# Entry to a gated MLP on one NeuronCore: order of evictions and sums, arithmetic moved from GpSimd to VectorE, six differences put off, the fourth product one step back

## The chip, the core and the metric

The kernel runs on one core of a Trainium2 chip. The metric is the time of one execution on the device in microseconds, given as the median of several runs. The engines are named as the profile names them: PE is TensorE (PEld its weight loads), DVE is VectorE, ACT is ScalarE, POOL is GpSimd, SP the engine that issues most of the DMAs. Each engine works through its own queue in order and waits on semaphores of the others.

## What is computed

One layer of a decoder trunk over 1024 tokens of width 1024, all in float32: a token mixer (causal pooling and gated linear attention) and then a gated MLP with a causal convolution of width 3, each behind a root-mean-square norm that is scaled and shifted by a conditioning vector. The change lies at the end of the first part and in the second:

```python
        y = jnp.concatenate([y_pool, y_gla], axis=-1) @ w_out[l]
        x = x + g1[:, None, :] * y

        h = modulate(rmsnorm(x), sh2, sc2)
        x = x + g2[:, None, :] * conv_ffn(h, w_up[l], conv_w[l], conv_b[l], w_down[l])
    return rmsnorm(x) * final_norm

def conv_ffn(h, w_up, conv_w, conv_b, w_down):
    up = h @ w_up
    y = causal_conv_width_3(up, conv_w) + conv_b
    a, b = jnp.split(y, 2, axis=-1)
    return (jax.nn.silu(a) * b) @ w_down
```

The MLP's inner width `D_FF` is 2816, that is 22 blocks of 128 channels for `a` and 22 for `b`.

## The kernel before

Everything is held transposed: channels on the 128 partitions, tokens along the row. The 1024 tokens are two halves (`hf` 0 and 1) of `T` = 512. A float32 product is made of three matmuls of split operands: each operand is cut into a high part (a cast by ScalarE) and a low part (a subtraction by VectorE, the `wl`, `ws` and `xs` rows of the profile), and `mm3` adds high by high, high by low and low by high.

**Up-projection.** For block `i` of the 22, the four quarter problems (halves of the tokens by the blocks `a` and `b`, over two halves of the inner dimension) are done with seven products instead of eight, in the manner of Strassen and Winograd. A product is 12 matmuls. The kinds are numbered 1 to 7: kinds 1 and 2 accumulate in a bank `x`, 5 and 3 in a bank `z`, and `y` is started with a copy of product 1 (`seeded`) and accumulates 6, 7 and 4. `up_step(kind, i)` issues one product and what follows it:

- after 5 and 6, ScalarE copies the bank out (`u[5]`, `u[6]`);
- after 3 and 7, VectorE adds bank and copy into `cb` (the eviction of line 944); after 7 the convolution of `cb` follows (`conv`: one ScalarE and two VectorE instructions) and gives `yb`;
- after 4, ScalarE copies `y` into `ca`; then come the convolution of `ca`, SiLU on ScalarE, the product with `yb` on VectorE (line 996) and a store of the result to DRAM, `gd[i]`, issued by GpSimd;
- last, for the first 11 blocks, GpSimd takes the difference of the two halves of the gated result and stores it (`s3d`); for the other 11 it loads the second half of block `i - 11` again, adds the second half of this one, and stores that (`s1d`). The down-projection reads both.

`order` is the order of the products on TensorE, which is written out by hand: TensorE's queue keeps it (`manual_schedule`). The queues of the other engines are ordered by a planner from priorities and its own estimate of when operands are ready; `issue_after` puts an instruction behind another on its engine. The first `RAMP` = 6 blocks begin with their products 1 and 2, which need the first half of the tokens alone, while the operands of the others are still being made from the second half (`norm2_second`, two steps of it after each product). Then the six blocks get their products 5, 4 (of the block before), 6, 3, 7. The other 16 blocks run with seven products each. `prepare` makes the weights' operands four products ahead: the load of raw weights (`up_raw`, four buffers of 512 KB), the differences of weights that Strassen's scheme needs (line 812) and the split (`wsplit`, lines 801 and 802).

**Entry.** Before it, `jobs_out(1)` is the output projection for the second half of the tokens: four banks at a time, and after each bank's last matmul `evac(d, pp)`: VectorE evicts the bank with gate and residual into `x1` (line 693), SP stores it, for `d` from 4 on VectorE adds the scaled quarter operands into `sums` (line 698), ScalarE squares it and GpSimd adds the square to `nacc` (line 234, by `sumsq_step`; the last square is not added but goes to TensorE by itself). `rstd_of` sums `nacc` over the channels with TensorE and makes the norm factor with ScalarE (`Ln`, then `Exp`). The banks of `jobs_out` are handed on to the MLP (`psum["f"]`, eight banks).

**Buffers.** `cy` gives six tiles of 1024 columns for `ca`, `cb`, `yb` and the gated result; `small` gives seven of 512 columns for the copies and the reloaded halves.

**Down-projection.** After the last block the same kind of scheme runs over `gd`, `s1d`, `s3d` and `w_down`. Its first products are mixed with product 4 of the last block; its tiles lie where those of the up-projection were.

## Time and profile before

| | us |
|---|---|
| median of 3 runs | 1050.42 |
| lowest and highest | 1049.86, 1051.85 |
| the profiled execution | 1047.94 |
| its span | 1046.2 |
| TensorE busy in it | 1001.2 |
| VectorE busy | 854.6 |
| ScalarE busy | 549.2 |
| GpSimd busy | 190.5 |

The span runs from the first to the last instruction of the profiled execution. In rows of the timeline the first number is the start in microseconds, the second the duration; then engine, line, operation, output and inputs by the program's names, shapes and the count of merged instructions; in brackets the idle time of the engine before it and what ended it. In rows of waits the numbers are the total, the count and the longest. In rows of groups the two numbers behind the bar are the sum in microseconds and the mean in nanoseconds, then the idle time before them.

### The profile page before, as it was taken

The page shows a single profiled execution, that of the slowest core. Times are in us where ns is not written, and L with a number is a line of the kernel's source. Part 1 is how long each engine was busy: PE and PEld are TensorE (multiplying, and loading weights), DVE is VectorE, ACT ScalarE, POOL GpSimd, SP SyncE. Part 2 cuts the span into 40 slices and gives each one's busy share as a digit, 9 for nine tenths or more (in the row PEclk, how much of TensorE's full clock was granted, in tenths as well). Part 3 has the DMA queues.
Part 4 walks back from the last instruction along what each step waited for, and adds up shares of the span by engine and source line. Part 5 has one row for each costly group of instructions (what it writes and reads, how often), then busy time and mean ns, then how long its engine had stood idle before and what let it go on. Part 6 is the DMA issues. An engine that isn't in the chain of part 4 may idle for free.

```text
span 1046.2 us, 12684 instructions
## 1 busy us (share of the span) xinstructions
PE 1001.2 (96%) x4481; PEld 815.4 (78%) x4481; DVE 854.6 (82%) x1197; ACT 549.2 (52%) x888; POOL 190.5 (18%) x163
## 2 busy tenths in 40 slices
PE   7989999998999989999999999999999999999995
PEld 5768868886777768877888888888888788888874
DVE  7967899689988849999977788777776776988883
ACT  5465585442733547665555455555554544644442
POOL 3437203222141030011100101101001000200210
PEclk8999999999999999999999999999999999999998
DMA  8743232455487442233222222332334787223642
GB/s 315 258 151 111 81 110 83 149 174 182 149 280 262 155 167 81 86 137 129 105 99 91 105 102 107 131 111 101 111 111 151 272 283 240 101 81 111 201 141 81
DMA packets 60817, 154.21 MB, mean 147 GB/s; under 512 B 6641, under 2 KB 9809, under 8 KB 60754
## 3 DMA queue, kind: packets, MB, share of 16 engines
q1 hardware_dynamic: 54192, 134.00, 37.8%
q0 software_dynamic: 4928, 17.30, 4.3%
q10 hardware_dynamic: 1634, 2.10, 0.6%
q8 instruction: 35, 0.57, 0.2%
q14 instruction: 28, 0.23, 0.1%
HBM read 127.69 MB, written 25.69 MB: 147 GB/s over the span
## 4 chain that ended last, share of the span: by engine, by line
PE 62%; DVE 23%; DMA 5%; ACT 4%; issue 4%; POOL 2%; SPq 0%; POOLq 0%; ACTq 0%; DVEq 0%
PE dn L107 18%; PE upy L107 14%; PE upx L107 9%; PE upz L107 9%; PE pp L107 8%; DVE wl L153 3%; DVE ada L219 2%; DMA ada<-in_adaT_dram 2%; DVE xs L802 2%; DVE hl L275 2%; POOL le L347 1%; DVE la L376 1%; DVE ua L812 1%; DVE lq L359 1%; PE ss L107 1%
## 5 line engine op out<-in xcount | busy, mean ns | idle before, releaser
L107 PE MATMUL dn<-xs 128*128 128x512 f32 (+1 forms) x480 | 111.1, 386 | 1.7 <-DVE xs L802 1.3
L107 PE MATMUL dn<-ws 128*128 128x512 f32 x456 | 108.3, 394 | 2.3 <-DVE xs L1110 2.3
L107 PEld LDWEIGHTS dn<-xs 128*128 128x128 f32 x480 | 88.5, 188 | 21.1 <-DVE xs L802 2.1
L107 PEld LDWEIGHTS dn<-ws 128*128 128x128 f32 x456 | 86.7, 190 | 20.9 <-issue 2.7
L107 PE MATMUL upy<-sh,xs 128*128 128x512 f32 x264 | 86.6, 390 | 2.1 <-DVE cb L944 2.1
L107 PE MATMUL upy<-sh,ws 128*128 128x512 f32 x264 | 86.4, 389 | 0.0
L153 DVE TENSOR_TENSOR wl<-raw,wh 128x1024 fp32r<-128x1024 f32 (+1 forms) x50 | 64.2, 1285 | 27.1 <-ACT wh L152 26.8
L997 POOL DMA_DIRECT2D gd<-y x22 | 12.0, 546 | 375.7 <-DVE y L996 358.7
L107 PE MATMUL pp<-hh,wh 128*128 128x512 f32 x176 | 73.7, 419 | 2.7 <-ACT hh L274 1.4
L107 PE MATMUL pp<-hl,wh 128*128 128x512 f32 x176 | 70.8, 402 | 4.8 <-DVE hl L275 4.8
L107 PE MATMUL pp<-hh,wl 128*128 128x512 f32 x176 | 70.8, 402 | 2.6 <-DVE wl L153 2.6
L802 DVE TENSOR_TENSOR xs<-ua,xs 128x512 fp32r<-128x512 f32 x78 | 60.6, 782 | 14.8 <-ACT xs L801 14.8
L802 DVE TENSOR_TENSOR ws<-ua,ws 128x512 fp32r<-128x512 f32 x76 | 55.1, 727 | 15.7 <-ACT ws L801 15.7
L107 PE MATMUL upx<-hh,xs 128*128 128x512 f32 x192 | 62.8, 392 | 2.5 <-DVE x L693 2.5
L801 ACT CAST ws<-ua 128x512 fp32r<-128x512 f32 x76 | 47.0, 622 | 34.4 <-PE upy L107 17.2
L152 ACT CAST wh<-raw 128x1024 fp32r<-128x1024 f32 (+1 forms) x50 | 50.4, 1008 | 26.8 <-DMA raw<-in_w_out_dram 10.8
L801 ACT CAST xs<-ua 128x512 fp32r<-128x512 f32 x78 | 48.1, 622 | 30.5 <-PE upy L107 17.4
L812 DVE TENSOR_TENSOR ua<-ua 128x512 f32<-128x512 f32 x88 | 60.2, 687 | 2.1 <-DMA ua<-in_w_up_dram 0.3
L347 POOL TENSOR_TENSOR le<-b 128x512 f32<-128x512 f32 x24 | 37.1, 1549 | 134.1 <-DVE lq L359 53.8
L107 PE MATMUL upz<-sh,ws 128*128 128x512 f32 x184 | 60.4, 389 | 0.0
L937 DVE SCALAR_TENSOR_TENSOR y<-ca,vec,y 128x1023 f32<-128x1023 f32 (+1 forms) x44 | 56.3, 1280 | 4.3 <-ACT y L934 3.5
L107 PEld LDWEIGHTS upy<-sh,xs 128*128 128x128 f32 x264 | 49.5, 188 | 13.2 <-DVE cb L944 2.9
(261 smaller groups left out, 2521.2 us busy)
## 6 DMA issues: line engine op xcount, KB each, us to landing
ua<-in_w_up_dram SPq DMA_DIRECT2D x49, 512.0 KB, 3.4
ada<-in_adaT_dram SPq DMA_DIRECT2D x32, 512.0 KB, 3.4
gd<-y POOLq DMA_DIRECT2D x22, 512.0 KB, 2.9
raw<-in_w_qkru_dram SPq DMA_DIRECT2D x18, 512.0 KB, 3.3
da<-gd SPq DMA_DIRECT2D x36, 256.0 KB, 2.8
da<-in_w_down_dram SPq DMA_DIRECT2D x36, 256.0 KB, 3.4
raw<-in_w_out_dram SPq DMA_DIRECT2D x16, 512.0 KB, 4.4
x<-in_xT_dram SPq DMA_DIRECT2D x24, 256.0 KB, 4.3
```

What stands on the lines that cost most here:

```text
L107: pe.matmul(out=out, lhsT=lhsT, rhs=rhs, start=start, stop=stop, skip_group_check=more)
L152: act.copy(out=wh, in_=raw)
L153: dve.tensor_tensor(out=wl, in0=raw, in1=wh.bitcast(F32), op=ALU.subtract)
L219: dve.scalar_tensor_tensor(out=a, in0=a, scalar=1.0, in1=cb, op0=ALU.mult, op1=ALU.mult, accum_out=acc)
L275: mark["split"] = dve.scalar_tensor_tensor(out=l, in0=t, scalar=sh, in1=h.bitcast(F32), op0=ALU.add, op1=ALU.subtract)
L347: pool_e.tensor_tensor(out=e.rearrange("p (n h) -> p n h", n=nb), in0=b.rearrange("p (n h) -> p n h", n=nb), in1=bb[:, :, 0, h - 1:h].broa ...
L359: dve.tensor_tensor(out=ql.rearrange("p e (n h) -> p e n h", h=h), in0=q2.rearrange("p e (n two h) -> p e n two h", two=2, h=h)[:, :, :, 1 ...
L801: act.copy(out=h, in_=src)
L802: dve.tensor_tensor(out=l, in0=src, in1=h.bitcast(F32), op=ALU.subtract)
L812: eng.tensor_tensor(out=out, in0=a, in1=b, op=ALU.subtract)
L937: dve.scalar_tensor_tensor(out=y[:, sh:], in0=c[:, :S - sh], scalar=cw[j], in1=y[:, sh:], op0=ALU.mult, op1=ALU.add)
L997: nc.gpsimd.dma_start(out=gd[i], in_=ya)
```

## The change

In the entry, the four sums are issued together after the last eviction, and the additions of squares for `d` from 4 to 6 go to VectorE. The order on TensorE changes: in the ramp 5, 6, 4, 3, 7 instead of 5, 4, 6, 3, 7; in the later blocks 1, 5, 4, 2, 6, 3, 7 instead of 1, 4, 5, 2, 6, 3, 7 (product 4 is always that of the block before). What follows the convolution of `ca` (SiLU, gate product, store, difference or addition) is put off by `gated()` to the start of the next product 5 or 6, with SiLU behind the latest seed copy on ScalarE. Differences and additions of gated halves are done by VectorE. For the first six blocks the difference is left out at first; it is made six blocks later from two halves loaded from `gd`. SiLU's table is loaded right behind the norm factor's `Exp`. `norm2_second` starts after the second product instead of the first.

```diff
-        act.activation(out=r, in_=r, func=AF.Exp, scale=-0.5)
+        mark["exp"] = act.activation(out=r, in_=r, func=AF.Exp, scale=-0.5)
...
-            if hf and d >= 4:
-                sums[d - 4] = up_pool.tile([P, T], F32, tag="a22", name="s1", bufs=10)
-                dve.scalar_tensor_tensor(out=sums[d - 4], in0=x1[1][d],
-                                         scalar=modv[:, 32 + d:33 + d], in1=x1[1][d - 4],
-                                         op0=ALU.mult, op1=ALU.add)
...
-            nacc[hf] = sumsq_step(nacc[hf], d, x1[hf][d], pool_e, True, own)
+            nacc[hf] = sumsq_step(nacc[hf], d, x1[hf][d], dve if hf and d >= 4 else pool_e,
+                                  True, own)
+            if hf and d == 7:
+                for e in range(4):
+                    sums[e] = up_pool.tile([P, T], F32, tag="a22", name="s1", bufs=10)
+                    dve.scalar_tensor_tensor(out=sums[e], in0=x1[1][4 + e],
+                                             scalar=modv[:, 36 + e:37 + e], in1=x1[1][e],
+                                             op0=ALU.mult, op1=ALU.add)
...
     for i in range(NFF):
-        order += [(1, i)] if i >= RAMP else [(5, i)]
-        order += [(4, i - 1)] if i else []
-        order += [(5, i), (2, i)] if i >= RAMP else []
-        order += [(6, i), (3, i), (7, i)]
+        done = [(4, i - 1)] if i else []
+        if i < RAMP:
+            order += [(5, i), (6, i)] + done + [(3, i), (7, i)]
+        else:
+            order += [(1, i), (5, i)] + done + [(2, i), (6, i), (3, i), (7, i)]
...
         r = rstd_of(nacc[1], s2)
+        with tc.issue_after(mark["exp"].ins):
+            act.preload_act_table_set("silu_and_others")
...
-        act.copy(out=y, in_=src)
+        mark["seed"] = act.copy(out=y, in_=src)
...
         if kind == 5 and i < RAMP:
             u["y"] = seeded(u["s"], w[0][:, 0] if i < 3 else None)
+        if kind in (5, 6):
+            gated()
...
             ya = conv(u["ca"], i)
-            last = act.activation(out=ya, in_=ya, func=AF.Silu)
+            pend.append((i, ya, u["yb"]))
+            del st_u[i]
+            if i == NFF - 1:
+                gated()
+
+    def gated():
+        while pend:
+            i, ya, yb = pend.pop(0)
+            with tc.issue_after(mark["seed"].ins):
+                last = act.activation(out=ya, in_=ya, func=AF.Silu)
             if i == NFF - 1:
                 exp_ln(last)
-            dve.tensor_tensor(out=ya, in0=ya, in1=u["yb"], op=ALU.mult)
+            dve.tensor_tensor(out=ya, in0=ya, in1=yb, op=ALU.mult)
             nc.gpsimd.dma_start(out=gd[i], in_=ya)
-            if i < NFF // 2:
-                sub(pool_e, u["yb"][:, 0:T], ya[:, 0:T], ya[:, T:])
-                nc.gpsimd.dma_start(out=s3d[i], in_=u["yb"][:, 0:T])
+            if RAMP <= i < 2 * RAMP:
+                a, b = small("s3"), small("s3")
+                nc.sync.dma_start(out=a, in_=gd[i - RAMP][:, 0:T])
+                nc.sync.dma_start(out=b, in_=gd[i - RAMP][:, T:])
+                sub(dve, a, a, b)
+                nc.gpsimd.dma_start(out=s3d[i - RAMP], in_=a)
+            if i < RAMP:
+                pass
+            elif i < NFF // 2:
+                sub(dve, yb[:, 0:T], ya[:, 0:T], ya[:, T:])
+                nc.gpsimd.dma_start(out=s3d[i], in_=yb[:, 0:T])
             else:
                 t = small("s1")
                 nc.sync.dma_start(out=t, in_=gd[i - NFF // 2][:, T:])
-                pool_e.tensor_tensor(out=t, in0=t, in1=ya[:, T:], op=ALU.add)
+                add_to(t, t, ya[:, T:])
                 nc.gpsimd.dma_start(out=s1d[i - NFF // 2], in_=t)
...
-        for _ in range(2):
+        for _ in range(2 if n else 0):
             next(second, None)
```

## The prediction

> **What bounds the kernel now.** I read the page first: TensorE works 96% of the span, so only its idle time can be won, and a change to other engines counts where TensorE waits.

> ```profile
> span 1046.2 us, 12684 instructions
> PE 1001.2 (96%) x4481; PEld 815.4 (78%) x4481; DVE 854.6 (82%) x1197; ACT 549.2 (52%) x888; POOL 190.5 (18%) x163
> ```

> Next, busy times by stage: entry and ramp of the MLP (386 to 482), the steady up-projection (to 810), the step into the down-projection (to 830), its first part. The first two numbers of a row are its window and length; then TensorE, weight loads, VectorE, ScalarE, GpSimd.

> ```profile
> 386.00:482.00 96.00, 91.43 (x398) 74.08 (x397) 94.34 (x128) 61.53 (x99) 12.27 (x12) 1.00 0.31 106
> 482.00:810.00 328.00, 328.00 (x1448) 271.38 (x1447) 258.36 (x311) 176.28 (x261) 43.43 (x54) 1.00 0.32 111
> 810.00:830.00 20.00, 18.32 (x79) 14.29 (x78) 13.79 (x15) 11.31 (x16) 2.40 (x3) 1.00 0.70 234
> 830.00:975.00 145.00, 145.00 (x642) 120.05 (x641) 118.37 (x180) 71.15 (x128) 13.24 (x7) 1.00 0.51 169
> ```

> TensorE loses 4.57 us in the first window, 1.68 in the third, nothing in the other two, at a granted clock of 1.00. So 6.25 us is the ceiling of any gain here. VectorE is full in the ramp (94.34 of 96) and has 69.6 us free in the steady stage. TensorE's waits name the places:

> ```profile
> PE upx L107 <- DVE x L693: 2.5, 1, 2.5
> PE upy L107 <- DVE cb L944: 2.1, 2, 1.2
> PE dn L107 <- DVE xs L802: 1.3, 1, 1.3
> PE dn L107 <- ACT xs L801: 0.4, 1, 0.4
> ```

> All but the last wait for VectorE. The timelines of the three places follow, each beside the part of the change that touches it.

> **Part 1, the entry: evictions ahead of sums, three adds from GpSimd to VectorE.**

> ```profile
> 384.78 1.43 DVE L693 SCALAR_TENSOR_TENSOR x<-pp,modv,x 128x512 f32<-128x512 f32 x2 [2.38 <-PE pp L107]
> 385.57 1.37 ACT L230 ACTIVATE nsq<-x 128x512 f32<-128x512 f32 x2
> 386.13 2.42 DVE L698 SCALAR_TENSOR_TENSOR s<-x,modv,x 128x512 f32<-128x512 f32 x2
> 386.34 3.34 POOL L234 TENSOR_TENSOR nsa<-nsa,nsq 128x512 f32<-128x512 f32 x2 [14.81 <-ACT nsq L230]
> 386.39 0.39 PE L107 MATMUL pp<-yh,wl 128*128 128x512 f32 x1
> 388.47 1.40 DVE L693 SCALAR_TENSOR_TENSOR x<-pp,modv,x 128x512 f32<-128x512 f32 x2
> 389.27 0.50 PE L107 MATMUL upx<-hh,xs 128*128 128x512 f32 x1 [2.48 <-DVE x L693]
> ```

> The first MLP matmul starts at 389.27, when the third eviction ends (388.47 plus half of the pair, 0.7). That eviction queues behind two sums of 2.42 us, stretched by GpSimd's adds: a pair of evictions, operations of the same kind, takes 1.40, so the stretch is about 1.0. Without the sums the third eviction follows the pair at 386.2 and ends at 386.9; TensorE, whose last matmul ends at 386.78, goes on at 387.0. Gain 389.27 - 387.0 = 2.3 us. The bounds: the moved adds (0.68 each, the price of a VectorE addition of that size below) may enter between the evictions, because their squares (the ScalarE pair from 385.57) are ready by then: two of them leave 1.0; the whole wait is 2.48. I take 2.3: the third eviction becomes ready at 386.2, about when the first square does. The four sums then follow; their reader needs the norm factor, which comes after the adds and one product later in TensorE's order than now.

> The stage's VectorE account: three adds are 3 x 0.68 = 2.0 us more; gone are two stretches at the sums, about 2.1 us. It comes out even.

> **Part 2, the ramp: six GpSimd half-differences go, the fourth product goes one step back.**

> ```profile
> 462.33 0.39 PE L107 MATMUL upy<-sh,xs 128*128 128x512 f32 x1
> 463.82 2.20 DVE L802 TENSOR_TENSOR xs<-ua,xs 128x512 fp32r<-128x512 f32 x1
> 464.16 1.30 POOL L812 TENSOR_TENSOR y<-y 128x512 f32<-128x512 f32 x1
> 465.94 0.68 DVE L944 TENSOR_TENSOR cb<-upy,u 128x512 f32<-128x512 f32 x1
> 466.67 0.50 PE L107 MATMUL upy<-sh,xs 128*128 128x512 f32 x1 [1.24 <-DVE cb L944]
> 481.41 0.50 PE L107 MATMUL upy<-sh,xs 128*128 128x512 f32 x1 [0.85 <-DVE cb L944]
> ...
> 487.14 2.72 PE upz L107 x12
> ...
> L802 DVE TENSOR_TENSOR xs<-ua,xs 128x512 fp32r<-128x512 f32 x15 | 13.3, 895 | 0.0
> L802 DVE TENSOR_TENSOR ws<-ua,ws 128x512 fp32r<-128x512 f32 x15 | 11.7, 781 | 0.0
> ...
> 435.33 0.59 ACT L951 COPY upy<-sp 128x512 f32<-128x512 f32 x1 [0.84 <-PE upy L107]
> ```

> Product 7 ends at 462.72. Its eviction (L944) reads the bank that product 4 goes on accumulating in, so TensorE may not start product 4 before it. It runs at 465.94, behind a weight split that takes 2.20 us while GpSimd's difference runs (1.30) and 0.68 otherwise: 1.52 lost. The two groups of splits between 395 and 482 show three such blocks (gate products 0 to 2): 13.3 + 11.7 - 30 x 0.68 = 4.6 us of VectorE. Without its own block this eviction would end at 465.1. And product 4 starts one product later, 2.7 us of further grace. Against both stands that TensorE comes 2.3 us earlier from part 1. Balance: needed at 466.67 - 1.24 - 2.3 + 2.7 = 465.8; there at 466.6 - 3.0 (its own block and that of gate product 0) = 463.6. A margin of 2.2 us, so both waits go: gain 1.24 + 0.85 = 2.1. The bounds run from that to a loss (first rival).

> What the step back moves closer: product 6 now follows 5, and its seed copy must be there. The copy of 435.33 starts with product 5 and ends 0.6 us into its 2.7: cost 0 by that cover, 0.6 for each of six if ScalarE came late. The gate's SiLU and multiply are issued one or two products later and hold two `cy` buffers longer; in the fourth ramp iteration seven of six are asked for, and a copy or a convolution waits for a multiply. TensorE's banks are evicted by other instructions, with two products of time: 0, or once a product, 2.7, if an eviction is caught.

> The preload brings one ScalarE table load of 1.28 us (row below) from the ramp to just after the norm factor, where ScalarE is 64% busy in the window. At most the first split operand comes 1.3 us later, and twelve products (33 us) stand ahead of its reader: 0, or 1.3 if that lead were gone.

> **Part 3, the steady stage: later differences and sums on VectorE, six pairs of halves loaded again.**

> ```profile
> L812 DVE TENSOR_TENSOR ua<-ua 128x512 f32<-128x512 f32 x64 | 44.0, 689 | 1.6
> L802 DVE TENSOR_TENSOR xs<-ua,xs 128x512 fp32r<-128x512 f32 x58 | 44.0, 761 | 14.8 <-ACT xs L801 14.8
> L802 DVE TENSOR_TENSOR ws<-ua,ws 128x512 fp32r<-128x512 f32 x58 | 41.5, 716 | 15.4 <-ACT ws L801 15.4
> ...
> 607.68 0.42 SPq L1003 DMA_DIRECT2D s<-gd  x1
> 634.46 1.30 POOL L1004 TENSOR_TENSOR s<-s,y 128x512 f32<-128x512 f32 x1
> ...
> s<-gd SPq DMA_DIRECT2D x11, 256.0 KB, 3.6
> ```

> Added to VectorE in the window: 5 differences, 6 late ones, 10 additions, 21 x 0.69 = 14.5 us. Taken away: the stretch of the splits, 44.0 + 41.5 - 116 x 0.69 = 5.5. Net +9 us against 69.6 free: load 79% to 82%. Cost 0. SP issues 12 loads more, 12 x 0.42 = 5 us of queue time over 110 us, and the pairs' data were written six gate products earlier. GpSimd keeps only its DMA issues; six stores merely move. VectorE now waits for loads at the head of its own queue; the row of 607.68 shows a load issued 26.8 us ahead of its use, landing in 3.6, so that wait is 0.

> **Part 4, the step into the down-projection.**

> ```profile
> 823.21 1.28 ACT L184 ACT_TABLE_LOAD   x1
> 823.23 1.22 DVE L996 TENSOR_TENSOR y<-y 128x1024 f32<-128x1024 f32 x1 [0.26 <-ACT y L993]
> 825.16 2.00 DVE L802 TENSOR_TENSOR xs<-rb,xs 128x512 fp32r<-128x512 f32 x1 [0.71 <-ACT xs L801]
> 825.31 1.29 POOL L1004 TENSOR_TENSOR s<-s,y 128x512 f32<-128x512 f32 x1
> 827.21 0.50 PE L107 MATMUL dn<-xs 128*128 128x512 f32 x1 [1.30 <-DVE xs L802]
> ```

> The last GpSimd addition stretches a split from 0.68 to 2.00, and TensorE waits 1.30. On VectorE the addition fits into the 0.71 us idle ahead of the split. Gain 1.3; 0.6 if it goes behind the wrong neighbour. The wait for ScalarE (0.4) stays.

> **Sum.** 2.3 + 2.1 + 0 + 1.3 = 5.7 us. The profiled execution took 1047.94 us (span 1046.2, 1.7 around it), so 1042.2 for it; it lies 2.5 under the median of 1050.42, so 1044.7 as a median. The bounds of the terms alone, 1.0 + 2.1 + 0.6 to 2.5 + 2.1 + 1.3, give 1044.5 to 1046.7; another microsecond either way for the spread of the runs (1049.86 to 1051.85).

> **Rivals.**

> *VectorE waits for weights in the ramp (1048.2).* Product 4's split frees the buffer of a coming weight tile; moved back, it stands two products ahead of its next user, not three.

> ```profile
> 452.30 3.91 DMA ua<-in_w_up_dram
> ...
> DVE ua L812 <- DMA ua<-in_w_up_dram: 0.3, 1, 0.3
> ```

> Now the 3.9 us are covered but for 0.3. With two splits alone as cover (1.3) each of four loads costs 2.6: 10.4, less the 4.6 of the blocks, less 2.7 of grace: TensorE loses 3.1 to 3.5 there, not 2.1. Gain 5.7 - 3.5 = 2.2. For: VectorE is full. Against: convolution steps lie between as well.

> *VectorE is simply full (1046.8).* If the ramp's splits are slow for another cause than GpSimd, the work taken over leaves VectorE as full as before, the 2.1 us stay, and 5.7 - 2.1 = 3.6 is left. For: 94.34 of 96. Against: 2.20 beside a GpSimd difference, 0.68 without one. [...]

> *Waits for the loaded halves in the steady stage (slower, about 1064).* If the loads are issued only when their user's turn is near, VectorE idles at the head of its queue in 16 places. Its free time, 69.6 - 9, allows 3.8 us for each; from 4.2 on the loss eats the 5.7. At 5 us (landing 3.6 and two weight issues ahead) TensorE loses 16 x 1.2 = 19, and 1044.7 + 19 = 1064. For: 3.6 is near the limit. Against: the 26.8 us of lead.

> *It does not change the order, or the waits come back (1049 to 1051).* VectorE's queue is the planner's, not the code's: two evictions ran ahead of two sums although the code alternates them. The adds could go ahead of evictions, and the earlier TensorE could meet the full VectorE later. Against: VectorE's own account is 4.6 us lighter.

> **Chances.** Forecast 0.60 (own range 1043.3 to 1046.9), ramp loads 0.12, full VectorE 0.06, no gain 0.10, steady waits 0.12. A measurement here tells 0.2%, 2.1 us, from nothing. Half of the second case and most of the fourth are under that: faster 0.72, same 0.15, slower 0.13. The range runs towards the no-gain case: 1043.0 to 1050.0.

> **What would show it.** Right: first MLP matmul within 0.8 us of the last `pp` one; no wait for L944; no split over 1 us where GpSimd worked; TensorE idle under 1 us between 386 and 482. Wrong: VectorE idle for `ua` in the ramp, or for the loaded halves later.

## The result, and the profile after

Eight runs of each kernel: 1043.78 us median with the change (1041.26 to 1046.16), 1050.14 before (1048.32 to 1056.59). The ratio is 0.9932 with an interval of 0.9915 to 0.9949: 7.1 us less, between 5.4 and 8.9. The profiled execution took 1042.56 us, its span 1040.8.

The stages of the changed kernel (columns as before):

```profile
386.00:482.00 96.00, 95.78 (x419) 78.37 (x419) 91.61 (x134) 65.28 (x104) 1.77 (x3) 1.00 0.30 105
482.00:810.00 328.00, 328.00 (x1449) 271.81 (x1448) 264.58 (x332) 174.73 (x257) 21.01 (x39) 1.00 0.35 124
810.00:830.00 20.00, 20.00 (x88) 15.88 (x87) 14.76 (x21) 13.23 (x20) 1.08 (x2) 1.00 0.81 293
830.00:975.00 145.00, 145.00 (x639) 119.83 (x638) 119.09 (x180) 71.78 (x129) 13.25 (x7) 1.00 0.49 165
```

Of 6.25 us of TensorE's idle time in these stages 0.22 is left. Its waits from the entry on:

```profile
PE dn L107 <- DVE xs L1131: 2.4, 1, 2.4
PE upx L107 <- DVE x L693: 0.2, 1, 0.2
```

The waits for the eviction in the ramp and at the step into the down-projection are gone; the wait of 2.4 near the end was there before (2.3) and is outside the change. The entry in the timeline:

```profile
385.81 2.17 DVE L693 SCALAR_TENSOR_TENSOR x<-pp,modv,x 128x512 f32<-128x512 f32 x3 [2.62 <-PE pp L107]
...
387.42 0.39 PE L107 MATMUL pp<-yh,wl 128*128 128x512 f32 x1
...
387.89 0.68 DVE L234 TENSOR_TENSOR nsa<-nsa,nsq 128x512 f32<-128x512 f32 x1
388.03 0.50 PE L107 MATMUL upx<-hh,xs 128*128 128x512 f32 x1 [0.22 <-DVE x L693]
...
388.49 0.74 DVE L693 SCALAR_TENSOR_TENSOR x<-pp,modv,x 128x512 f32<-128x512 f32 x1
```

Three evictions run in a row, the first moved add comes behind the third, and TensorE goes on after 0.22 us. The groups of weight splits on the page show what GpSimd's leaving did to VectorE: 688 and 689 ns on average, where they were 782 and 727.

```profile
L804 DVE TENSOR_TENSOR xs<-ua,xs 128x512 fp32r<-128x512 f32 x78 | 53.0, 688 | 14.6 <-ACT xs L803 14.6
L804 DVE TENSOR_TENSOR ws<-ua,ws 128x512 fp32r<-128x512 f32 x76 | 52.1, 689 | 14.6 <-ACT ws L803 14.5
```

And the step into the down-projection, where the last addition (line 946) fits in ahead of the split that used to take 2.00:

```profile
818.60 1.22 DVE L1010 TENSOR_TENSOR y<-y 128x1024 f32<-128x1024 f32 x1
...
819.85 0.69 DVE L946 TENSOR_TENSOR s<-s,y 128x512 f32<-128x512 f32 x1
...
820.46 0.69 DVE L804 TENSOR_TENSOR xs<-rb,xs 128x512 fp32r<-128x512 f32 x1
```

From the last matmul of the output projection to the end it is 659.8 us before (1046.2 - 386.39) and 653.4 after (1040.8 - 387.42): 6.4 less in these two executions. The three places give 2.3, 2.1 and 1.7; for the rest, 0.3, there is one candidate in the timelines: the first two matmuls after a wait start 0.33 us apart and not 0.23, and three such waits are gone. The runs say 7.1. What a wait can cost beyond its own length, in executions other than these two, is found below.

### The profile page after: what moved, and what is told of

Same layout as the page of the kernel before. It is cut to its first block, busy times and chain, and to the rows that moved or that the text cites. A ratio compares the mean times of both kernels' runs of the same rounds, so it can differ in the third digit from the quotient of the medians.

```text
span 1040.8 us, 12692 instructions
## 1 busy us (share of the span) xinstructions
PE 1000.3 (96%) x4481; PEld 815.7 (78%) x4481; DVE 854.7 (82%) x1222; ACT 549.8 (53%) x888; POOL 155.9 (15%) x138
## 4 chain that ended last, share of the span: by engine, by line
PE 75%; DVE 14%; ACT 3%; DMA 3%; issue 2%; POOL 1%; SPq 0%; POOLq 0%; ACTq 0%; DVEq 0%
PE dn L107 19%; PE upy L107 17%; PE pp L107 12%; PE upx L107 12%; PE upz L107 11%; DVE wl L153 3%; PE sc L107 2%; DVE hl L275 2%; DVE ada L219 2%; DMA raw<-in_w_out_dram 1%; DVE lb L219 1%; POOL le L347 1%; DVE la L376 1%; PE ss L107 1%; ACT wh L152 1%
## 5 line engine op out<-in xcount | busy, mean ns | idle before, releaser
L107 PE MATMUL dn<-xs 128*128 128x512 f32 (+1 forms) x480 | 110.8, 386 | 0.0
L107 PE MATMUL dn<-ws 128*128 128x512 f32 x456 | 108.3, 394 | 2.4 <-DVE xs L1131 2.4
L107 PEld LDWEIGHTS dn<-xs 128*128 128x128 f32 x480 | 88.6, 188 | 19.1 <-DVE xs L804 0.8
L107 PEld LDWEIGHTS dn<-ws 128*128 128x128 f32 x456 | 86.7, 190 | 20.9 <-issue 2.8
L107 PE MATMUL upy<-sh,ws 128*128 128x512 f32 x264 | 86.4, 390 | 0.0
L107 PE MATMUL upy<-sh,xs 128*128 128x512 f32 x264 | 86.4, 390 | 0.0
L107 PE MATMUL pp<-hl,wh 128*128 128x512 f32 x176 | 71.4, 406 | 6.2 <-DVE hl L275 6.2
L107 PE MATMUL pp<-hh,wh 128*128 128x512 f32 x176 | 74.2, 422 | 1.2 <-ACT hh L274 0.7
L107 PE MATMUL pp<-hh,wl 128*128 128x512 f32 x176 | 71.2, 405 | 2.7 <-DVE wl L153 2.7
L804 DVE TENSOR_TENSOR xs<-ua,xs 128x512 fp32r<-128x512 f32 x78 | 53.0, 688 | 14.6 <-ACT xs L803 14.6
L804 DVE TENSOR_TENSOR ws<-ua,ws 128x512 fp32r<-128x512 f32 x76 | 52.1, 689 | 14.6 <-ACT ws L803 14.5
L107 PE MATMUL upx<-hh,xs 128*128 128x512 f32 x192 | 62.8, 392 | 0.2 <-DVE x L693 0.2
L107 PE MATMUL upz<-sh,ws 128*128 128x512 f32 x184 | 60.5, 389 | 0.0
L939 DVE SCALAR_TENSOR_TENSOR y<-cb,vec,y 128x1023 f32<-128x1023 f32 (+1 forms) x44 | 56.4, 1281 | 3.5 <-ACT y L936 3.5
L107 PE MATMUL pp<-yh,wh 128*128 128x512 f32 x128 | 52.9, 413 | 5.5 <-DVE x L693 2.6
## 6 DMA issues: line engine op xcount, KB each, us to landing
da<-gd SPq DMA_DIRECT2D x36, 256.0 KB, 2.8
da<-in_w_down_dram SPq DMA_DIRECT2D x36, 256.0 KB, 3.4
x<-in_xT_dram SPq DMA_DIRECT2D x24, 256.0 KB, 4.6
```

The lines of the kernel that those rows point to most:

```text
L107: pe.matmul(out=out, lhsT=lhsT, rhs=rhs, start=start, stop=stop, skip_group_check=more)
L804: dve.tensor_tensor(out=l, in0=src, in1=h.bitcast(F32), op=ALU.subtract)
L939: dve.scalar_tensor_tensor(out=y[:, sh:], in0=c[:, :S - sh], scalar=cw[j], in1=y[:, sh:], op0=ALU.mult, op1=ALU.add)
```

## The experiments

Ratios are to the kernel before, timed on the same chip. Theory throughout: each of the three places was worth its wait, and GpSimd's arithmetic and the order of evictions made the waits.

**One part alone.** The entry alone (the hunk of `evac` and the start of `norm2_second`):

```diff
-            nacc[hf] = sumsq_step(nacc[hf], d, x1[hf][d], pool_e, True, own)
+            nacc[hf] = sumsq_step(nacc[hf], d, x1[hf][d], dve if hf and d >= 4 else pool_e,
+                                  True, own)
+            if hf and d == 7:
+                for e in range(4):
...
```

> The kernel before with the entry alone changed: the four sums behind the last eviction, the three adds on VectorE, the operand work one product later. Theory (VectorE's account sets the ramp's end): TensorE starts the MLP 2.3 us earlier, but VectorE's work up to the ramp's evictions is even (2.0 us added, 2.1 of stretch gone), so the eviction that product 4 waits for comes no earlier and the waits at line 944 grow from 2.1 to about 4.4 us; the time stays within 0.5 us of before. Rival (the terms simply add): the ramp's waits stay at 2.1 and the time falls by 2.3 us.

Measured: 0.9958 (0.9943 to 0.9972), 4.4 us faster. The ramp's waits did not grow:

```profile
PE upy L107 <- DVE cb L946: 1.3, 3, 0.7
...
PE upx L107 <- DVE x L693: 0.2, 1, 0.2
```

The theory missed here: the waits for the eviction fell from 2.1 to 1.3 although TensorE came 2.3 us earlier. VectorE's account was a little better than even: 93.67 us busy between 386 and 482, where it was 94.34. The rival's 2.3 us is too small as well; 0.8 of the rest is what the ramp's waits lost.

The arithmetic alone (`sub(pool_e, ...)` and `pool_e.tensor_tensor` of gated halves to `dve`, the first six from DRAM):

> The kernel before with GpSimd's differences and additions of gated halves given to VectorE and the first six differences made later from DRAM; entry and order as before. Theory (GpSimd's operations stretch VectorE's splits): no split over 1 us in the ramp, the eviction of 465.94 about 3 us earlier, both waits for it gone, the wait of 1.30 at the step into the down-projection gone, the entry's 2.48 left: 3.4 to 3.8 us faster. Rival (VectorE is simply full): the ramp's 2.1 us of waits stay, only the last one goes, 1.3 to 1.7 us faster.

Measured: 0.9964 (0.9950 to 0.9979), 3.8 us faster. The waits from the entry on:

```profile
PE dn L107 <- DVE xs L1118: 2.5, 1, 2.5
PE upx L107 <- DVE x L693: 2.5, 1, 2.5
PE dn L107 <- ACT xs L801: 0.8, 1, 0.8
```

Both ramp waits are gone without any step back; at the step into the down-projection 0.8 for ScalarE is left. That VectorE is simply full is refuted: it does the work itself and is on time.

The step back alone (the order, `gated()`, SiLU behind the seed):

> The kernel before with the fourth product a step back and the gate's SiLU and multiply put off; entry, preload and GpSimd's arithmetic as before. Theory (the wait is the short distance from product 7's eviction to product 4): the splits stay stretched to 2.2 us, but 2.7 us of grace cover lateness of 1.24 and 0.85, both ramp waits go; entry 2.48 and exit 1.7 stay: 2.1 us faster. Rival (VectorE falls behind for good in the ramp, 4.6 us of blocks): the waits only come a block later, under 1 us faster.

Measured: 1.0037 (1.0018 to 1.0056), 3.9 us slower. Both theories missed. The timeline of its costliest wait:

```profile
519.55 1.28 DVE L802 TENSOR_TENSOR xs<-ua,xs 128x512 fp32r<-128x512 f32 x2
...
520.49 2.70 POOL L812 TENSOR_TENSOR y<-y 128x512 f32<-128x512 f32 x1
...
523.67 2.59 DVE L935 SCALAR_TENSOR_TENSOR y<-ca,vec,y 128x1023 f32<-128x1023 f32 x2
...
526.35 1.06 ACT L1003 ACTIVATE y<-y 128x1024 f32<-128x1024 f32 x1 [4.25 <-DVE y L935]
527.32 0.57 ACT L984 COPY u<-upy 128x512 f32<-128x512 f32 x1
...
527.94 0.50 PE L107 MATMUL upy<-sh,ws 128*128 128x512 f32 x1 [2.61 <-ACT u L984]
```

The put-off SiLU stands in ScalarE's queue ahead of the copy of product 6's bank. It waits 4.25 us for a convolution that VectorE does late, and the copy, for which TensorE's product 7 waits 2.61, stands behind it. From the entry on TensorE's waits come to 1.2 us more than before, and in this execution the clock was halved behind the wait of 2.61, which cost 1.7 (such dips are the subject of the experiments on waits below).

**The order without the put-off gate:**

```diff
-        order += [(1, i)] if i >= RAMP else [(5, i)]
-        order += [(4, i - 1)] if i else []
-        order += [(5, i), (2, i)] if i >= RAMP else []
-        order += [(6, i), (3, i), (7, i)]
+        done = [(4, i - 1)] if i else []
+        if i < RAMP:
+            order += [(5, i), (6, i)] + done + [(3, i), (7, i)]
+        else:
+            order += [(1, i), (5, i)] + done + [(2, i), (6, i), (3, i), (7, i)]
```

> The kernel before with the order of products changed alone: product 4 one step back, and the gate (SiLU, multiply, GpSimd's difference or addition) at once behind it as before; entry and arithmetic as before. Theory (what made the step back alone slower is the put-off SiLU, which stands in ScalarE's queue ahead of the copy that product 7 waits for): no wait for a ScalarE copy, the ramp's two waits for line 944 gone by the step's grace of 2.7 us, 2.1 us faster than before. Rival (the order itself, or the tiles it holds longer, makes the waits): a wait of 2 to 3 us for a copy or an eviction around the end of the ramp, no gain or slower.

Measured: 1.0007 (0.9993 to 1.0021).

```profile
PE upy L107 <- ACT u L984: 1.8, 1, 1.8
...
PE upy L107 <- ACT upy L952: 1.1, 1, 1.1
...
524.11 1.06 ACT L994 ACTIVATE y<-y 128x1024 f32<-128x1024 f32 x1 [2.74 <-DVE y L938]
525.08 0.57 ACT L984 COPY u<-upy 128x512 f32<-128x512 f32 x1
```

The two waits for the eviction did go, as the grace of 2.7 us promised, but TensorE waits for ScalarE instead: 1.1 for the seed copy that product 6 now follows directly, 1.8 for a copy. So the order gains nothing by itself. The theory missed: SiLU (524.11) stands ahead of the copy here too, although nothing is put off, and waits 2.74 for a late convolution. With the gate put off the same place costs 2.6 instead of 1.8, and the ratio is higher by 0.0030, with an interval of about 0.0024 either way. That the put-off gate makes the step back slower is likely from this; TensorE's waits in the up-projection differ by 0.4 us only, 3.3 against 2.9, and what makes up the rest is not shown.

**One part undone.** The change without the new entry:

> The changed kernel with the entry as it was: sums between the evictions, the three adds on GpSimd, operand work from the first product on. Theory (each of the three places was worth its own wait, and a wait of TensorE brings a dip of the granted clock of 1.7 us in some executions): the 2.5 us wait for the third eviction returns, the ramp keeps no wait (its margin is 2 us and more), 2.3 to 4.0 us slower than the changed kernel, 0.9955 to 0.9970 of before. Rival (the entry's gain is absorbed by the full VectorE): under 1 us slower.

Measured: 0.9972 (0.9955 to 0.9988); against 0.9932 that is 4.2 us for the entry, with an interval of about 2.5 either way. The wait of 2.5 us is back, the ramp has none. The change without the step back and the put-off gate:

> The changed kernel with the order of products as before and the gate's SiLU, multiply and what follows done at once; entry, preload, arithmetic on VectorE and the late six differences as changed. Theory (GpSimd's blocks made the eviction late, the step back is only grace): needed at 463.1 on the clock of the profile before, there at 463.6: waits of 0 to 1 us at product 4, 0 to 1 us slower than the changed kernel. Rival (the short distance itself makes the waits): 2 us or more slower.

Measured: 0.9928 (0.9906 to 0.9951): no difference that can be told (about 3 us either way), and no wait in the ramp. The change with the arithmetic left on GpSimd:

> The changed kernel with all differences and additions of gated halves on GpSimd, the first six at once and in the tile of the second convolution. Theory (with the gate put off, the six tiles of 1024 columns are short: the tile is held until GpSimd's difference and its store are done, ScalarE's next convolution waits at the head of its queue, and a copy that TensorE waits for stands behind it): a wait of 2 to 3 us for a ScalarE copy in the ramp as with the step back alone, and 1.3 to 1.7 us at the step into the down-projection: 3.5 to 6 us slower than the changed kernel. Rival (that wait came from the entry or from GpSimd's blocks of VectorE alone): only the last place, 1.3 to 1.7 us.

Measured: 0.9997 (0.9980 to 1.0015): nothing is left of the gain; TensorE waits 2.6 us for a ScalarE copy as with the step back alone, 1.5 for evictions, 1.6 at the step into the down-projection. The explanation by the wide tiles was then put to the test by giving the difference a tile of its own:

```diff
-                sub(pool_e, yb[:, 0:T], ya[:, 0:T], ya[:, T:])
-                nc.gpsimd.dma_start(out=s3d[i], in_=yb[:, 0:T])
+                t = small("s3")
+                sub(pool_e, t, ya[:, 0:T], ya[:, T:])
+                nc.gpsimd.dma_start(out=s3d[i], in_=t)
```

> The changed kernel with the arithmetic on GpSimd, as in the run without the arithmetic, but the difference goes into a tile of 512 columns and no longer into that of the second convolution, which is free as soon as the multiply is done. Theory (the shortage of the six wide tiles makes ScalarE wait): ScalarE's waits for GpSimd's difference and its store in the ramp go, with them TensorE's 2.6 us wait for a copy; left are at most 1.5 us for evictions and 1.3 to 1.7 at the step into the down-projection: 2.6 us faster than that run, 0.9970 to 0.9980 of before. Rival (GpSimd's blocks of VectorE make it): the wait of 2.6 us stays, 0.9997 of before.

Measured: 1.0040 (1.0023 to 1.0057), slower still. ScalarE's waits for GpSimd's difference (3.5 us) and its store (2.3) are gone, as expected, but

```profile
PE upy L107 <- ACT u L988: 7.8, 6, 1.9
```

TensorE's waits for the copy are there six times. The shortage of wide tiles is real, but it is not what costs TensorE its time here: a late instruction ahead of the copy in ScalarE's queue is. The first wait (1.9 us) and the other five (1.2 each):

```profile
519.17 1.06 ACT L1007 ACTIVATE y<-y 128x1024 f32<-128x1024 f32 x1 [3.47 <-DVE y L939]
...
542.76 0.62 ACT L803 CAST ws<-ua 128x512 fp32r<-128x512 f32 x1 [1.43 <-PE upz L107]
543.29 0.58 ACT L988 COPY u<-upy 128x512 f32<-128x512 f32 x1
...
543.92 0.50 PE L107 MATMUL upy<-sh,ws 128*128 128x512 f32 x1 [1.19 <-ACT u L988]
```

At the first it is SiLU, which waits 3.47 for a convolution. At the other five it is the cast of a weight, which waits 1.43 until a product has ended. Why the planner put that cast ahead of the copy in this kernel is not shown. The change with the first six differences at once, on VectorE:

```diff
-            if i < RAMP:
-                pass
-            elif i < NFF // 2:
+            if i < NFF // 2:
```

> The changed kernel with the first six differences made at once by VectorE from the gated result, not later from DRAM; the rest as changed. Theory (the tiles of 1024 columns are what the delay buys): the tile of the second convolution is held for the 2 to 3 us until its store has landed, ScalarE's convolutions wait, TensorE waits 0.5 to 2.6 us in the ramp: 0.5 to 3 us slower than the changed kernel. Rival (only VectorE's load counts, 0.69 us more of 13.6 us in each ramp iteration, and it has some free now): no wait, no difference.

Measured: 0.9925 (0.9902 to 0.9948): no wait, and no difference that can be told (about 3 us either way); a gain from the reload is not shown. The change with the last addition on GpSimd (`pool_e if i == NFF - 1 else dve`):

> The changed kernel with the very last addition of gated halves, block 21, given back to GpSimd. Theory: one weight split at the step into the down-projection is stretched from 0.68 to 2.0 us and TensorE waits 1.3 us for it there, 0.4 more for ScalarE; nothing else moves: 1.3 to 1.7 us slower than the changed kernel, 0.9945 of before. Rival (the 1.7 us there went because the loads landed in another order): no wait over 0.5 us, no difference.

Measured: 0.9948 (0.9929 to 0.9966), 1.7 us more than the change. The interval of that difference, about 2.6 either way, does not tell it from nothing; the waits in the trace do:

```profile
PE dn L107 <- DVE xs L804: 1.3, 1, 1.3
PE dn L107 <- ACT xs L803: 0.7, 1, 0.7
```

One GpSimd instruction brings back both waits at that place, the one for ScalarE too.

**The two parts that count, and nothing else.** The new entry and `dve` for `pool_e` in the differences and additions, at once:

> The kernel before with two things alone: the entry of the change, and all differences and additions of gated halves on VectorE, at once. No step back, no put-off gate, no reload of the first six, no preload. Theory (these two carry the gain, the rest is needed only where GpSimd keeps the arithmetic): no wait in the ramp, none over 0.5 us at the step into the down-projection, the time within 1 us of the changed kernel, 0.9920 to 0.9940 of before. Rival (the step back and the reload each hide part of a full VectorE): waits of 1 to 3 us at line 944 in the ramp, 0.995 of before.

Measured: 0.9921 (0.9898 to 0.9945). The two alone multiply to 0.9958 x 0.9964 = 0.9922. One wait of 0.6 for an eviction is left in the ramp, and 0.6 at the step into the down-projection; the time cannot be told from the change's.

**Do waits cost more than themselves?** Two executions with the same entry wait of 2.5 us, the windows around it:

```profile
386.00:396.00 10.00, 7.52 (x30) 5.21 (x29) 9.19 (x12) 5.52 (x10) 4.86 (x3) 1.00 0.44 154
```

is the kernel before, with a granted clock of 1.00, and the arithmetic alone has 0.83:

```profile
391.00:401.00 10.00, 7.52 (x23) 5.10 (x22) 8.50 (x11) 4.66 (x8) 4.84 (x3) 0.83 0.43 157
```

that is 1.7 us of 10 lost to a dip of the clock behind the wait. To see whether waits bring such dips, product 4 was put directly behind product 7 in the 16 steady blocks of the simple kernel:

```diff
-        order += [(1, i)] if i >= RAMP else [(5, i)]
-        order += [(4, i - 1)] if i else []
+        order += [(4, i - 1), (1, i)] if i >= RAMP else [(5, i)]
+        order += [(4, i - 1)] if 0 < i < RAMP else []
```

> The kernel 'simple' with product 4 of the block before directly behind its product 7 in the steady blocks, so that TensorE waits for the eviction of product 7 in 16 places where it had no wait. Theory (a wait of TensorE of about 1 us or more can bring a dip of the granted clock that costs 1.7 us): besides 16 waits of 0.8 to 1.5 us, some dips appear between 530 and 805, where ten profiles show none; the time grows by the sum of the waits and 1.7 us for each dip, 15 to 35 us slower than 'simple'. Rival (the dips come by themselves, by the time of the program): waits but no dips there, the time grows by the waits alone, 13 to 24 us.

Measured: 1.0097 (1.0067 to 1.0127), 1062.41 us against 1044.13 for the simple kernel.

```profile
PE upy L107 <- DVE cb L946: 14.7, 17, 2.2
```

Between 530 and 805 there are 13 waits of 0.8 us at most and no dip: at this length the rival's forecast held. The one dip in the steady blocks, at 506, follows the wait of 2.2. Then the same with the eviction of product 7 done four times over:

```diff
-            add_to(u["cb"][:, T:], pp, u[5])
+            for _ in range(4 if i >= RAMP else 1):
+                add_to(u["cb"][:, T:], pp, u[5])
```

> As 'waits' (product 4 directly behind product 7 in the steady blocks), with the eviction of product 7 done four times over, the same numbers each time, so that TensorE waits longer in the same 16 places. Theory (a wait of TensorE brings a dip of the granted clock of 1.7 us only from a length between 0.9 and 1.3 us on, and then in some places): waits of 2.5 to 3 us each and 4 to 16 dips between 530 and 805, each 1.7 us. Rival (the dips come by themselves at certain times of the program): the same long waits and no dip there.

Measured: 1.0787 (1.0762 to 1.0812), 1133.3 us.

```profile
530.00:885.00 355.00, 306.21 (x1208) 246.02 (x1209) 245.69 (x313) 145.87 (x216) 15.14 (x28) 0.91 0.23 81
```

In its timeline the first matmuls after a wait:

```profile
554.00 0.79 PE L107 MATMUL upy<-sh,ws 128*128 128x512 f32 x1 [3.49 <-DVE cb L946]
...
555.02 1.05 PE L107 MATMUL upy<-sh,ws 128*128 128x512 f32 x2
555.87 0.63 PE L107 MATMUL upy<-sl,ws 128*128 128x512 f32 x1
556.30 1.05 PE L107 MATMUL upy<-sh,ws 128*128 128x512 f32 x2
```

Three matmuls take 1.28 us (555.02 to 556.30), where they take 0.68 otherwise. Behind each of the 16 waits (15 of 3.5 us and the first of 2.2, 54.4 in sum) lies such a dip, 1.7 us lost in 12 places and 3.4 in four: 34 us. The waits grew by 40.6 against the kernel with the short ones, the dips by 32; the time by 70.9. That the dips come by themselves is refuted.

**A version beyond the change.** The simple kernel with the first half's adds on VectorE too, and the first half's output stores issued by GpSimd:

```diff
-            nacc[hf] = sumsq_step(nacc[hf], d, x1[hf][d], dve if hf and d >= 4 else pool_e,
+            nacc[hf] = sumsq_step(nacc[hf], d, x1[hf][d], dve if d >= 4 else pool_e,
...
-            (nc.scalar if k % 4 else nc.sync).dma_start(
+            (nc.gpsimd if hf == 0 else nc.scalar if k % 4 else nc.sync).dma_start(
```

> The kernel 'simple' with two things more, outside the change: the adds of squares of the first half's norm, from the fifth on, on VectorE too, and the first half's output stores issued by GpSimd instead of SP and ScalarE. Theory (SP's queue stands 4 us at a store that waits for its output; the loads behind it land late and hold VectorE, whose eviction TensorE waits for at the last product): the last wait of 2.4 us and the dip of the clock behind it go or halve, and the wait for the norm's sum (0.9 us) goes: 2 to 5 us faster than 'simple'. Rival (the loads are late because stores and loads share the DMA engines): the wait stays over 2 us, under 1 us faster.

Measured: 0.9913 (0.9892 to 0.9934), 1043.12 us. It is the lowest ratio measured, but the interval does not tell it from the change. The wait of 0.9 us for the norm's sum is gone; the late wait is not:

```profile
PE dn L107 <- DVE xs L1112: 2.1, 1, 2.1
```

SP no longer stands behind a store, yet VectorE still waits 4.1 us for loads there. The theory was wrong about what delays them; what does was not followed further.

## Why the prediction was right or wrong

**The forecast's size.** It said 5.7 us and 1044.7; the medians moved by 6.4, the ratio says 7.1, and the change lies at the low edge of the range given (0.9932 of 1050.14 is 1043.0). Faster was right, the sum was short, though the interval of 5.4 to 8.9 takes in 5.7. The step that failed is the sum, in two places. The step into the down-projection was put at 1.3 with "The wait for ScalarE (0.4) stays"; both waits went, 1.7, and one GpSimd addition brings both back. And each wait was priced at its own length alone; what it does to the clock was put at nothing, without a reason. The execution that was read had no dip at the entry nor at the step into the down-projection; of five profiles with the entry's wait of 2.5 us three had one, of seven with a wait of 1.3 us at the other place four. At 1.7 us each that is about 2 us on average, an estimate from these counts. With the 6.4 of the two profiles it makes 8.4, inside the interval. The prediction also noted that the execution it read lay 2.5 us under the median, and drew nothing from it. Whether dips make that gap is not shown: its mean granted clock, 0.989, lies among those of the other runs of that kernel (0.979 to 0.994). The range's low end had no term behind it: the bounds and the microsecond of spread give 1043.5, not 1043.0.

**Entry.** Right to a tenth: the third eviction sets the start, TensorE waits 0.22. The adds came between the third and the fourth eviction, where they cost nothing. In time the two experiments give 4.4 us (about 1.5 either way) and 4.2 (about 2.5). That is more than the wait of 2.3; the dips behind it, 1.0 on average by the count above, and the 0.8 that the ramp's waits lost in the first of them would make up most of the rest.

**GpSimd's blocks.** Right: with the arithmetic on VectorE no split is stretched (between 386 and 482 the longest of the change took 0.71 us) and the ramp's waits are gone, with the step back (the change) and without it (two runs).

**The step back.** Wrong. "A margin of 2.2 us" counted 2.7 for it; the margin was not needed, and by itself the order trades 2.1 us of waits for 2.9. The sentence that failed is the one that covered product 6's seed copy with product 5's 2.7 us: the copy can be late in ScalarE's queue, and TensorE waited 1.1 for it. The put-off gate was priced by the buffers it holds and not by its place in that queue: the step "TensorE's banks are evicted by other instructions" overlooked that the copies of products 5 and 6 are such instructions and stand behind SiLU. In the change itself SiLU still waits for a convolution, 3.2 us at the longest in the ramp, but TensorE waits for no copy behind it.

**Steady stage.** Right, the account a little too high: VectorE went from 258.4 to 264.6 us where +9 was forecast, no TensorE wait; the loads of halves held nobody.

**The rivals.** Ramp loads: VectorE waited 1.5 us once for a weight load, TensorE never. Full VectorE: refuted by the arithmetic alone. Steady waits and no gain: did not come.

## What to carry to other kernels

Read which instruction stands ahead of the late one in its engine's queue, and whose instruction runs beside it: here one GpSimd operation of 1.3 us cost VectorE 1.3 to 1.5 us, and TensorE up to 1.3. Price a put-off instruction by what stands behind it in its new place, not only by the buffers it holds. And here a wait of TensorE could cost more than itself: of the 44 steps of 3.41 us (last section) in which it was idle for 1.5 us or more, 39 were followed by a dip of the clock, which cost 1.7 us or more, and the one execution that was read showed none at the entry nor at the step into the down-projection. So look at several executions before summing waits.

## What the runs showed of the hardware

In the 16 profiles, from 386 on and up to the last product's end, each dip of TensorE's granted clock came behind a wait: none behind waits of 1.24 us or less (60 of them), 11 behind 18 waits of 1.3 to 2.7 us at the entry, in the up-projection and at the step into the down-projection, 13 behind 16 waits of 2.1 to 2.5 near the end, 15 behind 15 of 3.5. In a dip the granted clock was 0.50 for 3.41 us, or for 6.83, and half of that time was lost, 1.7 or 3.4 us.

```profile
385.28:388.70 3.42, 1.50 (x7) 0.92 (x5) 3.42 (x5) 2.55 (x5) 2.28 (x2) 1.00 0.61 230
388.70:392.11 3.41, 2.84 (x12) 2.36 (x13) 3.41 (x4) 1.23 (x2) 2.58 (x2) 1.00 0.41 154
...
390.49:393.90 3.41, 1.09 (x5) 0.56 (x3) 3.41 (x4) 2.16 (x4) 2.69 (x2) 1.00 0.41 154
393.90:397.31 3.41, 3.25 (x8) 2.58 (x9) 3.41 (x5) 1.23 (x2) 2.15 (x2) 0.50 0.42 154
```

In the first, 1.92 us of the wait fall into one step and the clock stays at 1.00; in the second it is 2.32, and the next step runs at 0.50. The waits of 1.3 us brought a dip in the four profiles in which a wait for ScalarE, or part of it, lay in the same step, and in none of the three in which it did not.

GpSimd and VectorE took longer beside each other, in both directions: in the kernel before, VectorE's split at 463.82 took 2.20 us beside GpSimd's difference of 1.30, and such a split took 0.68 otherwise; in the step back alone, where VectorE was already at work (519.55), GpSimd's difference at 520.49 took 2.70 and not 1.30.
